# A transformer trunk on one core: norm gains applied later, fp32 router logits, and a new order of the experts' weight chunks

## The chip, the core and the metric

The kernel runs on one core of a Trainium2 chip. The metric is the device time of one execution in microseconds (us), the median over several runs. Engines are named as in the profile: PE (TensorE), DVE (VectorE), ACT (ScalarE), POOL (GpSimd), and SP, which here only issues transfers.

## What is computed

The reference is a trunk of two layers over 256 latent and 256 context tokens of width 1024. Each layer: modulation by a conditioning vector (adaLN), four token mixers, a gated merge, and a layer norm; then a channel mixer and a second layer norm. The channel mixer is a dense SwiGLU network of width 3584 in layer 0 (called FFN here) and a mixture of eight such experts in layer 1 (MoE), two per token. Layer 1 computes only the latent tokens. The part that the change touches:

```python
y, yc = _token_mixing(...)
x = _layer_norm(ALPHA * x + mod[2] * y, ln1_g[layer], ln1_b[layer])
f = _channel_mixer(x * (1.0 + mod[4]) + mod[3], layer, ...)
x = _layer_norm(ALPHA * x + mod[5] * f, ln2_g[layer], ln2_b[layer])
...
def _moe_swiglu(h, w_router, w1, w3, w2):
    top_v, top_i = lax.top_k((h @ w_router).astype(jnp.float32), TOP_K)
    gates = jax.nn.softmax(top_v, axis=-1)
    ...  # each expert's rows: (silu(h @ w1) * (h @ w3)) @ w2
```

## The kernel before, in words

**Weights.** All large weights come from memory in chunks of 512 KB (`Flow.load`, L135, issued by SP into a ring of `wr` buffers). fp32 products are made from two reduced-precision parts: ACT copies a chunk to `wh` (L266), DVE subtracts to get the rest `wl` (L253), and PE multiplies hi by hi, hi by lo and lo by hi. The operations go through small helpers, so most have a helper's line: matmul L246, transpose L250, tensor-tensor L253, tensor-scalar L258 and L260, fused L263, activation L266. The class `Flow` holds the list of steps of a stage. Before each step it issues what it can ahead: loads while a raw buffer is free, casts while a cast buffer is free and the chunk either is used within `look` steps or should have arrived by an estimate (`c.ready`). The engines take their operations in the order in which the program issues them.

**The first norm of a layer** is `out_norm` (L1412). The output projection gives four tiles of 128 tokens in layer 0 (latent and context) and two in layer 1. For each tile: half of the statistics in `second`, then `normed` (aggregate on DVE, the power -1/2 on POOL, scaling on ACT and DVE), then `third`, eight PE transposes whose results ACT and DVE scale and shift into `hraw` and split into `Bh` and `Bl`, the input of the next stage. Since that scale and shift already contain the norm's gain and bias, `x` itself is needed much later, for the residual sum; still, step `fourth` computes it there with two POOL operations on 128 x 1024 (`residual`, L799): `lnr<-lnr,gbc` and `x<-lnr,bbc`. In layer 0 a string of letters sets the order of the steps per tile: `sthrn` is second, transposes of the tile before, its residual, norm; `e` is an early half of the FFN's first matmuls.

**The FFN** (`ffn`) has seven groups of four column blocks, each with two halves of PE work. After a half, `fill(1)` lets one more block of the adaLN projection be made: two chunks, 16 small matmuls on PE or three multiply-and-add stages on POOL. `between` runs pieces of other work. `rest` ends with the final norms of the four tiles; `fill(96)` ahead of them issues what is left of the adaLN blocks.

**Router.** In layer 1 `route` multiplies the split input with the split router weights (32 matmuls per two tiles with `wrs`), copies the logits to SBUF, turns them round with four small matmuls, and takes the two largest of eight; `as_rows` turns the input back into token rows for the gather. Then counts (`pc`), positions (`pp`), the experts' order by size and the choice of one of three programs follow. SP loads the experts' first chunks (L2363) once the order is known.

**MoE.** Experts are sorted by tokens into eight slots. The run shown takes the program with 256, 192, 128, 64, 32, 32, 32, 32 tokens at most. Slots 0 to 2 are *hot*: their chunks are cast and multiplied in three products. Slots 3 to 7 are *cold*: raw fp32 chunks are used as the stationary side, in many short matmuls (`mps<-wr,Xs`, `yps<-wr,mhs`). Every slot has 84 chunks, 672 in all. `merged` puts hot and cold chunks in one sequence, two at a time: after a first run of 14 cold chunks it takes a hot pair when the summed cost is at or below the mean so far, else a cold pair. The cost of a chunk is a table by the slot's tokens: 3.75 n/128 up to 128 tokens, else 3 per full 128 and 2 for a rest. A tail that is written out by hand closes the sequence. A slot's input is gathered by matmuls with one-hot rows (`pg<-ohs` for the small slots together, `pg<-oh` for a hot slot); `need(order[0], 2)` has two of the eight column groups of the small gather made before the first chunk, the rest come between chunks.

Of the kernel before, what the change touches and what calls it, by code (L numbers as in the profile page):

```python
# [17 lines left out]
P = 128  # L18
# [65 lines left out]
class Flow:  # L84
# [9 lines left out]

    def step(self, fn, take=(), drop=None):
        self.steps.append((fn, list(take), list(take) if drop is None else list(drop)))
# [129 lines left out]
class Trunk:  # L226
# [1185 lines left out]
    def out_norm(self, l, Mh, Ml, streams, Nh, Nl, x, load, early=()):  # L1412
# [34 lines left out]
        def first(k2):  # L1447
            if k2 == 0:
                z.ps = [self.bank("SB"[t // 2], [512]) for t in range(nt)]
            for t in range(nt):  # L1450
                block(z.ps[t], t, k2, cs[0][k2])
            if k2 == 2 and l:

                for q in (z.g, z.b):
                    self.act(q, q, AF.Copy, scale=ALPHA)
# [22 lines left out]
        def normed(t):  # L1478
            z.x[t] = self.norm_rows(z.p, z.r[t], z.st[t], z.r[t])
# [18 lines left out]
        def fourth(t):  # L1498
            s, i = tiles[t]
            self.residual(z.x[t], z.g, z.b, x[s][:, i])  # L1500
# [4 lines left out]
        def last():  # L1505

            second(1, (0, 1, 2))
            raw(0, 0, (0, 0, 0, 0))
            second(1, (3,))
            raw(0, 1, (0, 0, 0, 0))  # L1510
            for h in range(2):
                high(0, h)
            normed(1)
            for h in range(2):
                low(0, h)
            raw(1, 0, LAST)
# [11 lines left out]
        else:  # L1528

            k012, k3 = (0, 1, 2), (3,)  # L1530
            ops = {"s": lambda t: second(t, k012), "t": lambda t: second(t, k3), "n": normed, "h": third, "r": fourth}
            for t in range(nt + 1):
                for o in "stn" if t == 0 else "sthrn" if t < nt else "eehr":
                    if o == "e":
                        early.pop(0)()
                    else:
                        i = t - (o in "hr")
                        step(lambda o=o, i=i: ops[o](i), cs[1] if o == "s" else [], cs[1] if (o, i) == ("t", nt - 1) else [])
            for f in early:
                f()  # L1540
# [4 lines left out]
    def ffn(self, Hh, Hl, Nh, Nl, x, during, between, late):  # L1545
# [13 lines left out]
        def up(f):  # L1559
# [21 lines left out]
            def rest():  # L1581
                step(a, cs[0:1])
                self.fill(1)
                step(b, cs[1:2])
                self.fill(1)
                between()
# [70 lines left out]
        def rest():  # L1657
# [16 lines left out]

            for i, t in enumerate((2, 3, 0, 1)):
# [7 lines left out]
            for i, f in enumerate(late):  # L1683
                if i == 4:
                    step(lambda: third(1))
                f()
            step(lambda: z.l.release())
# [9 lines left out]
    def body(self, out):  # L1697
# [109 lines left out]
        def during(g):  # L1807
# [10 lines left out]
            if g > 2 and not pieces and not hasattr(pz, "gone"):  # L1818
                pz.gone = True
                step(lambda: pz.z.pool.release())  # L1820
                pz.room = fl.more("rd", 2, 2, "left")
            if g == 7:
                pz.room()
# [5 lines left out]
        early, rest = self.ffn(Mh, Ml, Mh, Ml, x, during, between, [u[0] for u in s5u + M1.nak + M1.naq])  # L1829
        pz.room = self.out_norm(0, Mh, Ml, (0, 1), Mh, Ml, x, load, early)  # L1830
        self.todo = [z for l, i in TODO for z in self.blocks(l, i)]
# [11 lines left out]
        pz.room = self.out_norm(1, Nh, Nl, (1,), Nh, Nl, x, lambda: None, [lambda t=t: self.route(t, B.h, B.l) for t in range(2)])  # L1843
# [16 lines left out]
    def router(self):  # L1860
# [8 lines left out]

        R.w = T([8, 16], "wrs", F32R)  # L1870
        self.split(R.w[:, :, 0:8], R.w[:, :, 8:16], self.wrt)
        R.add = T([8], "radd")
        self.tt(R.add[:16], self.ident[:16, 0:8], self.ident[:16, 8:16], ALU.add)
# [7 lines left out]
    def route(self, t, Bh, Bl):  # L1881

        R, v = self.R, self.nc.vector
        c = slice(t * P, (t + 1) * P)
        if t == 0:
            R.pl = self.bank("V", [272])
        pl = R.pl
# [3 lines left out]
        if t == 0:  # L1891
            return
        lt = R.pool.tile([P, 256], F32, name="lgt")
        v.tensor_copy(lt[:16], pl[:16, 0:256])
        for t in range(2):
            self.mm(pl[:, 256 + t * 8:264 + t * 8], lt[:16, t * P:(t + 1) * P], R.add[:16], True, True)
        v.tensor_copy(R.lg, pl[:, 256:272].rearrange("p (a b) -> p a b", a=2))
        for t in range(2):
            v.max(R.mx[:, t], R.lg[:, t])
            v.max_index(R.ix[:, t], R.mx[:, t], R.lg[:, t])  # L1900
# [11 lines left out]
    def moe(self, Bh, Bl, xs, out):  # L1912
# [17 lines left out]
        self.tt(sel, m1, m2, ALU.add)  # L1930

# [8 lines left out]
        for t in range(2):  # L1940
            self.as_rows(t, Bh, Bl)
# [391 lines left out]
        def merged(caps, hot, cold):  # L2333
# [31 lines left out]
        for nm, caps, hot, cold in paths:  # L2365
            with contextlib.ExitStack() as arm:
# [13 lines left out]
                gb = []  # L2380
# [10 lines left out]
                def step():  # L2391
# [19 lines left out]
                def one(q, i, c):  # L2411
# [7 lines left out]
                    if q < 12 or q % 3 == 2:  # L2419
                        step()  # L2420
# [15 lines left out]
                need(order[0], 2)  # L2436
# [174 lines left out]
```

## Time and profile before

| | us |
|---|---|
| median of 3 runs | 2531.98 |
| lowest and highest run | 2526.71, 2532.57 |
| the profiled execution | 2521.39 |
| its span, first to last instruction | 2519.5 |
| PE busy | 2331.8 (93%) |
| DVE, ACT, POOL busy | 1337.9, 897.7, 830.5 |
| layer-0 norm / FFN / layer 1's norm and router / MoE | from about 605 / 653 / 1530 / 1567 |

The mean granted clock of TensorE is 0.969 of full. The page's busy times are averages over the whole span; PE's 93% tells little of a stage of 50 us. Times in the rows below are us from the span's start. A timeline row gives start, busy time, engine, line, operation, output <- inputs, partitions x elements and, in brackets, how long the engine was idle before and what released it; `xN` is N alike instructions in one row.

### The profile page before, as it was taken

What the parts mean: (1) busy time and instruction counts of PE and PEld (TensorE: products, weight loads), DVE (VectorE), ACT (ScalarE), POOL (GpSimd) and SP (SyncE); (2) the same over time, 40 slices, a digit from 0 to 9 for tenths busy, and PEclk for the clock granted to TensorE, in tenths of its full rate; (3) what the DMA queues carried; (4) which work ended last, traced back from release to release, by engine and by line L of the source; (5) the groups of instructions that cost most, each with busy time, mean ns of one, the idle gap of its engine ahead of it and who ended that gap; (6) DMA issues with size and microseconds to landing.
All of it is one profiled execution on the core that took longest, in us unless ns stands there. A gap on an engine that the chain in (4) does not pass through costs nothing. (4 is left out here: it accounts for less than half of the span.)

```text
span 2519.5 us, 44047 instructions
## 1 busy us (share of the span) xinstructions
PE 2331.8 (93%) x16948; PEld 1798.9 (71%) x16948; DVE 1337.9 (53%) x2132; ACT 897.7 (36%) x1477; POOL 830.5 (33%) x1646
## 2 busy tenths in 40 slices
PE   7799999998899999998898887999999999999995
PEld 5566666876777778777776685667777777777663
DVE  4455564346424545567465647224444465557775
ACT  2533333323322422223343444222233333345561
POOL 5307883332132565552488754000000000000000
PEclk9999998999999999998998998999999999999998
DMA  7644112324343554451332342899999999999996
GB/s 269 207 134 139 52 58 71 106 82 167 102 143 128 168 185 171 156 182 49 103 126 68 96 163 84 319 361 395 384 397 388 398 348 362 395 380 404 407 408 273
DMA packets 167995, 556.21 MB, mean 221 GB/s; under 512 B 17472, under 2 KB 32608, under 8 KB 167776
## 3 DMA queue, kind: packets, MB, share of 16 engines
q1 hardware_dynamic: 156224, 543.33, 58.6%
q10 hardware_dynamic: 11552, 9.98, 1.2%
q8 instruction: 135, 2.21, 0.4%
q14 instruction: 84, 0.69, 0.1%
HBM read 543.32 MB, written 9.92 MB: 220 GB/s over the span
## 5 line engine op out<-in xcount | busy, mean ns | idle before, releaser
L253 DVE TENSOR_TENSOR wl<-wr,wh 128x1024 fp32r<-128x1024 f32 (+1 forms) x412 | 529.6, 1304 | 353.1 <-ACT wh L266 350.2
L266 ACT ACTIVATE wh<-wr 128x1024 fp32r<-128x1024 f32 x474 | 493.0, 1052 | 475.3 <-DMA wr<-in_moe_w_dram 264.1
L253 POOL TENSOR_TENSOR wide<-ymo,mbc 32x128 f32<-32x128 f32 (+1 forms) x28 | 18.7, 668 | 586.9 <-DVE ymo L253 522.3
L253 POOL TENSOR_TENSOR wl<-wr,wh 128x1024 fp32r<-128x1024 f32 x62 | 151.5, 2458 | 168.9 <-ACT wh L266 161.3
L246 PE MATMUL psA<-Bh,wh 128*128 128x256 f32 (+1 forms) x592 | 204.3, 345 | 1.3 <-ACT gt L266 1.3
L246 PE MATMUL psA<-Bh,wl 128*128 128x256 f32 (+1 forms) x592 | 197.7, 334 | 0.5 <-DVE wl L253 0.5
L246 PE MATMUL psA<-Bl,wh 128*128 128x256 f32 (+1 forms) x592 | 198.0, 334 | 0.0
L246 PE MATMUL mps<-wr,Xs 128*32 128x128 f32 (+1 forms) x4032 | 177.2, 290 | 9.2 <-DMA wr<-in_moe_w_dram 6.6
L246 PE MATMUL mps<-wh,X 128*128 128x512 f32 x560 | 179.9, 406 | 2.5 <-ACT wh L266 2.5
L246 PE MATMUL yps<-wh,mh 128*128 128x512 f32 x504 | 162.4, 403 | 2.4 <-ACT wh L266 2.3
L246 PEld LDWEIGHTS mps<-wr,Xs 128*32 128x32 f32 (+1 forms) x4032 | 122.8, 113 | 56.8 <-issue 23.8
L253 POOL TENSOR_TENSOR t<-H,a 128x32 f32<-128x32 f32 x512 | 151.0, 316 | 21.8 <-PE psV L246 2.3
L246 PE MATMUL psA<-Hh,wh 128*128 128x512 f32 x352 | 151.4, 430 | 6.4 <-ACT wh L266 5.4
L246 PE MATMUL psA<-Hl,wh 128*128 128x512 f32 x352 | 144.0, 409 | 0.0
L246 PE MATMUL psA<-Hh,wl 128*128 128x512 f32 x352 | 143.8, 408 | 0.1
L246 PEld LDWEIGHTS psA<-Bh,wh 128*128 128x128 f32 x592 | 116.2, 196 | 25.5 <-issue 6.8
L246 PE MATMUL psB<-wh,hid 128*128 128x512 f32 x384 | 123.1, 402 | 7.7 <-DVE y L253 7.7
L246 PEld LDWEIGHTS mps<-wh,X 128*128 128x128 f32 x560 | 102.2, 189 | 33.6 <-issue 5.0
L246 PEld LDWEIGHTS psA<-Bh,wl 128*128 128x128 f32 x592 | 115.9, 196 | 11.6 <-DVE wl L253 0.8
L246 PEld LDWEIGHTS psA<-Bl,wh 128*128 128x128 f32 x592 | 116.3, 196 | 9.8 <-issue 0.2
L246 PE MATMUL mps<-wl,X 128*128 128x512 f32 (+1 forms) x336 | 118.9, 402 | 4.0 <-DVE wl L253 3.9
L246 PEld LDWEIGHTS yps<-wh,mh 128*128 128x128 f32 x504 | 92.1, 188 | 29.9 <-ACT wh L266 4.9
(515 smaller groups left out, 4820.2 us busy)
## 6 DMA issues: line engine op xcount, KB each, us to landing
wr<-in_moe_w_dram SPq DMA_DIRECT2D x672, 512.0 KB, 8.0
wr<-in_w_ada_dram SPq DMA_DIRECT2D x96, 512.0 KB, 4.4
wr<-in_ffn_w_dram SPq DMA_DIRECT2D x84, 512.0 KB, 4.4
wr<-in_w_gate_dram SPq DMA_DIRECT2D x64, 512.0 KB, 3.5
wr<-in_w_in_dram SPq DMA_DIRECT2D x28, 512.0 KB, 3.7
wr<-in_w_branch_dram SPq DMA_DIRECT2D x16, 512.0 KB, 3.5
wr<-in_w_out_dram SPq DMA_DIRECT2D x16, 512.0 KB, 3.5
wr<-in_w_v_dram SPq DMA_DIRECT2D x8, 512.0 KB, 5.1
```

What stands on the lines that cost most here:

```text
L246: self.nc.tensor.matmul(out, w, x, start=start, stop=stop)
L253: (eng or self.nc.vector).tensor_tensor(out, a, b, op=op)
L266: self.nc.scalar.activation(out, a, f, **kw)
```

## The change

Five things change.

- **Residual of the first norms.** `normed` writes the normalised tile straight into `x`; the gain and bias rows are not loaded in `out_norm`. In layer 0 eight POOL operations on 128 x 1024 apply them to `x` inside the FFN, one with each `between`, after the pieces of the S5 work. In layer 1 two rows are loaded at the MoE's chunk 24 into the space that slot 2's input takes later, and at chunk 40 two ACT scalings and four POOL operations apply them; slot 2's gather may begin from chunk 120.
- **adaLN blocks.** `fill(2)` stands three times among the layer-0 norm steps (letter `f`), and the FFN fills only from its fifth column block on.
- **Quiet stretches.** In the layer-0 norms and in the FFN's final norms, a chunk that is first used more than ten steps later is not cast early.
- **Router.** Logits come from the unsplit `hraw` (fp32) and the unsplit router weights, 16 matmuls into 128 x 8, before the splits; copies and the turning matmuls go. `as_rows(0)` stands before the counts, `as_rows(1)` behind them.
- **MoE order.** The cost is 3.5 n/128 below 128 tokens (128 tokens cost 3), the first cold run is 6 chunks, and all eight column groups of the small gather are made before the first chunk.

```diff
@@ Flow.ahead
-                if c.raw or (r and (c.first <= self.now + self.look or self.tr.clock >= c.ready)):
+                if c.raw or (r and (c.first <= self.now + self.look or self.tr.clock >= c.ready and not self.later(c))):
...
+    def later(self, c):
+        return any(a <= self.now < b and c.first > self.now + 10 for a, b in self.quiet)
@@ out_norm
-            z.g, z.b = (p.tile([P, D], F32, name=n) for n in ("gbc", "bbc"))
-            self.rows(z.g, A['ln_rows'][l, 0])
-            self.rows(z.b, A['ln_rows'][l, 1])
...
         def normed(t):
-            z.x[t] = self.norm_rows(z.p, z.r[t], z.st[t], z.r[t])
+            s, i = tiles[t]
+            z.x[t] = self.norm_rows(z.p, z.r[t], z.st[t], x[s][:, i])
...
             raw(0, 1, (0, 0, 0, 0))
+            early[0]([z.raw[0, h] for h in range(2)])
...
             raw(1, 1, LAST)
-            early[0]()
+            early[1]([z.raw[1, h] for h in range(2)])
...
-            early[1]()
-            for t in range(2):
-                fourth(t)
...
-                for o in "stn" if t == 0 else "sthrn" if t < nt else "eehr":
+                for o in "stn" if t == 0 else "sthn" if t < nt - 1 else "stfhn" if t < nt else "eefhfee":
                     if o == "e":
                         early.pop(0)()
+                    elif o == "f":
+                        self.fill(2)
@@ ffn
-                self.fill(1)
+                self.fill(f > 3)
@@ body, during
+                for s in range(2):
+                    for i in range(2):
+                        for h, op in enumerate((ALU.mult, ALU.add)):
+                            pieces.append(lambda s=s, i=i, h=h, op=op: self.tt(x[s][:, i], x[s][:, i], pz.gb[h], op, nc.gpsimd))
@@ route
-        for k in range(8):
-            self.mm(pl[:16, c], R.w[:, k], Bh[:, k, c], k == 0, False)
-            self.mm(pl[:8, c], R.w[:, k, 0:8], Bl[:, k, c], False, k == 7)
...
+        for h, raw in enumerate(raws):
+            for k in range(4):
+                self.mm(R.pl[:, t], raw[:, k], self.wrt[:, h * 4 + k], h + k == 0, h + k == 4)
+        v.tensor_copy(R.lg[:, t], R.pl[:, t])
@@ moe
-                return 3.75 * n / P if n <= P else 3 * (n // P) + 2 * (n % P > 0)
+                return 3.5 * n / P if n < P else 3 * (n // P) + 2 * (n % P > 0)
-                i = 1 if len(seq) < 14 else 0 if sm <= mean * len(seq) else 1
+                i = 1 if len(seq) < 6 else 0 if sm <= mean * len(seq) else 1
...
+                        if s == 2 and q < 120:
+                            return
...
+                    if q == 40:
+                        for i, op in enumerate((ALU.mult, ALU.add)):
+                            self.act(ab[0][:, i], ab[0][:, i], AF.Copy, scale=ALPHA)
+                            for t in range(2):
+                                self.tt(xs[:, t], xs[:, t], ab[0][:, i], op, g)
...
-                need(order[0], 2)
+                need(order[0], 8)
```

DVE in the layer-0 norms, at tile 3 of 0 to 3, before: `lns` holds a tile's half statistics, `lnm` its mean and factors, `wl` is a weight chunk's low part, `Bl` the split of the tile before.

```order
L754 BN_STATS lns<-lnr_5499 128x6
L253 TENSOR_TENSOR wl<-wr,wh 128x1024 x3
L260 TENSOR_SCALAR hraw<-psB,affG,affB 128x128
L253 TENSOR_TENSOR Bl<-hraw,Bh 128x4x128
L260 TENSOR_SCALAR hraw<-psB,affG,affB 128x128
L253 TENSOR_TENSOR Bl<-hraw,Bh 128x4x128
L760 BN_AGGR lnm<-lns 128x2
```

And the same place with the change (its helpers' lines are 5 higher):

```order
L759 BN_STATS lns<-lnr_5495 128x6
L258 TENSOR_TENSOR wl<-wr,wh 128x1024
L265 TENSOR_SCALAR hraw<-psB,affG,affB 128x128
L258 TENSOR_TENSOR Bl<-hraw,Bh 128x4x128
L265 TENSOR_SCALAR hraw<-psB,affG,affB 128x128
L258 TENSOR_TENSOR Bl<-hraw,Bh 128x4x128
L765 BN_AGGR lnm<-lns 128x2
```

Two of the three casts stand behind the aggregate now.

DVE in the layer-1 norm, from tile 1's half statistics to the indices of the two largest logits, before:

```order
L754 BN_STATS lns<-lnr_14142 128x6
L760 BN_AGGR lnm<-lns 128x2
L258 TENSOR_SCALAR lnm<-lnm 128x1
L263 SCALAR_TENSOR_TENSOR lnm<-lnm 128x1
L260 TENSOR_SCALAR lnr_14142<-lnr_14142,lnm 128x512
L253 TENSOR_TENSOR Bl<-hraw,Bh 128x4x128 x2
L260 TENSOR_SCALAR hraw<-psB,affG,affB 128x128 x2
L253 TENSOR_TENSOR Bl<-hraw,Bh 128x4x128 x2
L1894 COPY lgt<-psV 16x256
L1897 COPY lg<-psV 128x16
L1899 MAX mx_14132<-lg 128x8
L1900 MAX_INDEX ix_14133<-mx_14132,lg 128x8
```

With the change:

```order
L759 BN_STATS lns<-lnr_14138 128x6
L1898 COPY lg<-psV 128x8
L1899 MAX mx_14132<-lg 128x8
L1900 MAX_INDEX ix_14133<-mx_14132,lg 128x8
L765 BN_AGGR lnm<-lns 128x2
L263 TENSOR_SCALAR lnm<-lnm 128x1
L268 SCALAR_TENSOR_TENSOR lnm<-lnm 128x1
L265 TENSOR_SCALAR x_5483<-lnr_14138,lnm 128x512
L258 TENSOR_TENSOR Bl<-hraw,Bh 128x4x128 x2
L265 TENSOR_SCALAR hraw<-psB,affG,affB 128x128 x2
L1898 COPY lg<-psV 128x8
L1899 MAX mx_14132<-lg 128x8
```

Tile 0's logits stand ahead of tile 1's aggregate, tile 1's ahead of the last two splits.

PE at the start of the MoE, before (`pg<-ohs` is the gather of the small slots, `pg<-oh` that of slot 0, `mps` a chunk's products):

```order
L246 MATMUL pg<-ohs,Bl 128x192 x2
L246 MATMUL mps<-wr,Xs 64x256 x4
L246 MATMUL pg<-ohs,Bh 128x192 x2
L246 MATMUL pg<-ohs,Bl 128x192 x2
L246 MATMUL pg<-ohs,Bh 128x192 x2
L246 MATMUL pg<-ohs,Bl 128x192 x2
L246 MATMUL mps<-wr,Xs 64x256 x4
```

With the change, from the last of eight such column groups:

```order
L251 MATMUL pg<-ohs,Bh 128x192 x2
L251 MATMUL pg<-ohs,Bl 128x192 x2
L251 MATMUL mps<-wr,Xs 64x256 x12
L251 MATMUL pg<-oh,Bh 128x256 x2
L251 MATMUL pg<-oh,Bl 128x256 x2
L251 MATMUL mps<-wr,Xs 64x256 x4
```

The eight column groups stand ahead of the first chunk.

## Rows read from the trace of the kernel before

**Rows 1.** Windows, four stretches: us, PE, PEld, DVE, ACT, POOL busy, PEclk, DMA share, GB/s.
```profile
605.00:653.00 48.00, 31.19 (x178) 27.70 (x177) 36.57 (x51) 22.05 (x41) 23.20 (x12) 0.86 0.18 55
...
1530.00:1587.00 57.00, 38.21 (x194) 29.49 (x192) 33.26 (x83) 16.23 (x35) 11.75 (x7) 0.70 0.37 140
...
1740.00:2270.00 530.00, 521.95 (x5590) 394.14 (x5588) 269.13 (x351) 191.78 (x248) 20.40 (x25) 1.00 0.98 382
...
2270.00:2490.00 220.00, 202.43 (x1914) 147.54 (x1913) 156.01 (x187) 110.35 (x129) 4.82 (x8) 1.00 1.02 407
```

**Rows 2.** Timeline, layer-0 norms, PE: start, us, operation, [idle before <-releaser].
```profile
611.19 1.97 PE L250 MATMUL psB<-in_small_dram,lnr 128*128 128x128 f32 x8 [5.58 <-ACT lnr L266]
...
621.09 1.10 PE L250 MATMUL psB<-in_small_dram,lnr 128*128 128x128 f32 x8 [1.99 <-ACT lnr L266]
...
630.12 1.18 PE L250 MATMUL psB<-in_small_dram,lnr 128*128 128x128 f32 x8 [2.41 <-ACT lnr L266]
...
645.25 1.97 PE L250 MATMUL psB<-in_small_dram,lnr 128*128 128x128 f32 x8 [6.83 <-ACT lnr L266]
```

**Rows 3.** Timeline, layer-0 norms, DVE and POOL at tiles 2 and 3.
```profile
631.43 2.37 POOL L253 TENSOR_TENSOR lnr<-lnr,gbc 128x1024 f32<-128x1024 f32 x1 [2.41 <-PE psB L250]
...
631.77 7.59 DVE L253 TENSOR_TENSOR wl<-wr,wh 128x1024 fp32r<-128x1024 f32 x3
...
633.89 3.25 POOL L253 TENSOR_TENSOR x<-lnr,bbc 128x1024 f32<-128x1024 f32 x1
...
646.18 1.22 DVE L253 TENSOR_TENSOR wl<-wr,wh 128x1024 fp32r<-128x1024 f32 x1 [1.25 <-ACT wh L266]
```

**Rows 4.** Windows, late FFN; timeline, POOL, the last adaLN block and the final norm's power.
```profile
1000.00:1070.00 70.00, 68.38 (x304) 55.43 (x303) 39.41 (x39) 18.27 (x21) 43.14 (x32) 1.00 0.49 171
...
1131.29 2.90 POOL L253 TENSOR_TENSOR wr<-wr,csil 128x1024 f32<-128x1024 f32 x1
...
1138.17 0.45 POOL L253 TENSOR_TENSOR ada<-wr 128x128 f32<-128x128 f32 x1
...
1146.62 0.57 POOL L253 TENSOR_TENSOR lnm<-lnm,mhalf 128x1 f32<-128x1 f32 x1 [8.00 <-DVE lnm L258]
```

**Rows 5.** Timeline, DVE at layer 0's first tile, then layer-1 norm and router.
```profile
610.13 0.16 DVE L263 SCALAR_TENSOR_TENSOR lnm<-lnm 128x1 f32<-128x1 f32 x1 [0.66 <-POOL lnm L253]
...
610.32 0.55 DVE L260 TENSOR_SCALAR lnr<-lnr,lnm 128x512 f32<-128x512 f32 x1
...
1547.69 2.29 DVE L263 SCALAR_TENSOR_TENSOR lnm<-lnm 128x1 f32<-128x1 f32 x1 [0.67 <-POOL lnm L253]
...
1550.01 2.66 DVE L260 TENSOR_SCALAR lnr<-lnr,lnm 128x512 f32<-128x512 f32 x1
...
1556.11 3.53 DVE L253 TENSOR_TENSOR Bl<-hraw,Bh 128x512 fp32r<-128x512 f32 x2
...
1559.70 0.27 PE L246 MATMUL psV<-Bl,wrs 128*8 128x128 f32 x1 [2.11 <-DVE Bl L253]
...
1564.02 0.56 PE L246 MATMUL pc<-sel,onesr 128*128 128x8 f32 x2 [1.89 <-DVE sel L253]
```

**Rows 6.** Timeline, PE, the first chunk and the fourth (of the four).
```profile
1573.88 1.98 PE L246 MATMUL mps<-wr,Xs 128*64 128x256 f32 x8 [0.72 <-DVE Xs L2086]
...
1587.50 2.81 PE L246 MATMUL mps<-wr,Xs 128*64 128x256 f32 x24 [0.58 <-ACT Xs L266]
```

**Rows 7.** Timeline, PE, chunks of 64, 32 and 192 tokens (two from 2002.23).
```profile
1712.52 5.40 PE L246 MATMUL mps<-wr,Xs 128*64 128x256 f32 x48
...
1806.44 1.95 PE L246 MATMUL mps<-wr,Xs 128*32 128x128 f32 x64
...
2002.23 0.73 PE L246 MATMUL mps<-wh,X 128*128 128x512 f32 x2
...
2007.09 1.08 PE L246 MATMUL yps<-wr,mhs 128*32 128x128 f32 x32
```

**Rows 8.** Waits of SP's queue, 1560 to 2519 us: total, times, longest.
```profile
SPq L135 <- PE mps L246: 189.3, 129, 9.8
```

More of the change, by code (lines that the diff above doesn't have):

```diff
@@ L93, in __init__ @@
         self.pre = pre
+        self.quiet = []
     def step(self, fn, take=(), drop=None):
@@ L1451, in first @@
                 block(z.ps[t], t, k2, cs[0][k2])
-            if k2 == 2 and l:
-                for q in (z.g, z.b):
-                    self.act(q, q, AF.Copy, scale=ALPHA)
             if k2 == 3:
@@ L1496, in low @@
             self.tt(lo, src, hi.bitcast(F32), ALU.subtract)
-        def fourth(t):
-            s, i = tiles[t]
-            self.residual(z.x[t], z.g, z.b, x[s][:, i])
         z.x, z.raw = {}, {}
@@ L1530, in out_norm @@
             k012, k3 = (0, 1, 2), (3,)
-            ops = {"s": lambda t: second(t, k012), "t": lambda t: second(t, k3), "n": normed, "h": third, "r": fourth}
+            ops = {"s": lambda t: second(t, k012), "t": lambda t: second(t, k3), "n": normed, "h": third}
+            a = len(self.flow.steps)
             for t in range(nt + 1):
-                for o in "stn" if t == 0 else "sthrn" if t < nt else "eehr":
+                for o in "stn" if t == 0 else "sthn" if t < nt - 1 else "stfhn" if t < nt else "eefhfee":
                     if o == "e":
                         early.pop(0)()
+                    elif o == "f":
+                        self.fill(2)
                     else:
-                        i = t - (o in "hr")
+                        i = t - (o in "h")
                         step(lambda o=o, i=i: ops[o](i), cs[1] if o == "s" else [], cs[1] if (o, i) == ("t", nt - 1) else [])
-            for f in early:
-                f()
+            self.flow.quiet.append((a, len(self.flow.steps)))
         step(lambda: z.p.release())
@@ L1686, in rest @@
                 f()
+            self.flow.quiet.append((a, len(self.flow.steps)))
             step(lambda: z.l.release())
@@ L1821, in during, with rows @@
                 pz.room = fl.more("rd", 2, 2, "left")
+                def rows():
+                    pz.gp = self.pool("ln0")
+                    pz.gb = [pz.gp.tile([P, D], F32, name=n) for n in ("gbc", "bbc")]
+                    for h in range(2):
+                        self.rows(pz.gb[h], A['ln_rows'][0, h])
+                step(rows)
+                for s in range(2):
+                    for i in range(2):
+                        for h, op in enumerate((ALU.mult, ALU.add)):
+                            pieces.append(lambda s=s, i=i, h=h, op=op: self.tt(x[s][:, i], x[s][:, i], pz.gb[h], op, nc.gpsimd))
+                            if h:
+                                pieces.append(lambda: None)
+                pieces.append(lambda: pz.gp.release())
             if g == 7:
@@ L1829, in body @@
         early, rest = self.ffn(Mh, Ml, Mh, Ml, x, during, between, [u[0] for u in s5u + M1.nak + M1.naq])
+        self.todo = [z for l, i in TODO for z in self.blocks(l, i)]
         pz.room = self.out_norm(0, Mh, Ml, (0, 1), Mh, Ml, x, load, early)
-        self.todo = [z for l, i in TODO for z in self.blocks(l, i)]
         rest()
@@ L1842, in body @@
         step(self.router)
-        pz.room = self.out_norm(1, Nh, Nl, (1,), Nh, Nl, x, lambda: None, [lambda t=t: self.route(t, B.h, B.l) for t in range(2)])
+        pz.room = self.out_norm(1, Nh, Nl, (1,), Nh, Nl, x, lambda: None, [lambda raws, t=t: self.route(t, raws) for t in range(2)])
         pz.room()
@@ L1879, in router, with route @@
         R.lg, R.mx, R.ix = T([2, 8], "lg"), T([2, 8], "mx8"), T([2, 8], "ix8", U32)
-    def route(self, t, Bh, Bl):
+    def route(self, t, raws):
         R, v = self.R, self.nc.vector
-        c = slice(t * P, (t + 1) * P)
         if t == 0:
-            R.pl = self.bank("V", [272])
-        pl = R.pl
-        for k in range(8):
-            self.mm(pl[:16, c], R.w[:, k], Bh[:, k, c], k == 0, False)
-            self.mm(pl[:8, c], R.w[:, k, 0:8], Bl[:, k, c], False, k == 7)
[L1891 to L1900, printed above, removed]
+            R.pl = self.bank("V", [2, 8])
+        for h, raw in enumerate(raws):
+            for k in range(4):
+                self.mm(R.pl[:, t], raw[:, k], self.wrt[:, h * 4 + k], h + k == 0, h + k == 4)
+        v.tensor_copy(R.lg[:, t], R.pl[:, t])
+        v.max(R.mx[:, t], R.lg[:, t])
+        v.max_index(R.ix[:, t], R.mx[:, t], R.lg[:, t])
     def as_rows(self, t, Bh, Bl):
@@ L1939, in moe @@
         self.mm(pp[:, 1], self.ones, sf[:, 0], False, True)
-        for t in range(2):
-            self.as_rows(t, Bh, Bl)
+        self.as_rows(1, Bh, Bl)
         pos, key, slot = T([2, 8], "pos"), T([8], "key"), T([8], "slot")
@@ L2389, in moe, with step @@
                 todo.insert(0 if order[0] in small else len(todo), (None, setup_small(small)))
-                def step():
+                def step(q):
                     if todo:
                         s = todo[0][0]
+                        if s == 2 and q < 120:
+                            return
                         if s is None or s in slots:
@@ L2419, in one @@
                     if q < 12 or q % 3 == 2:
-                        step()
+                        step(q)
+                    if q == 24:
+                        last = "X2" if caps[2] == P else "X3"
+                        ab.append(pool.tile([P, caps[2] // 64, D], F32, name="ab", tag=last, bufs=1))
+                        for i in range(2):
+                            self.rows(ab[0][:, i], A['ln_rows'][1, i])
+                    if q == 40:
[3 more added lines that the diff above has]
+                                self.tt(xs[:, t], xs[:, t], ab[0][:, i], op, g)
                     for _ in jobs[:1 if q < len(seq) - 8 else 3 * (q < len(seq) - 1)]:
```

10 lines of the change are left out of this document (4 added, 6 removed).

## Prediction

> **What bounds the kernel now.** I read the windows view first, stage by stage, since TensorE's 93% of the whole span hides where it waits. [Rows 1] are the four stretches that the change touches. In the layer-0 norms (605 to 653 us) PE works 31.2 of 48 us, in the layer-1 norm and router (1530 to 1587 us) 38.2 of 57: there PE waits for a chain of small DVE, ACT and POOL operations. In the experts (MoE) PE works 522 of 530 us up to 2270, while the transfers run at 382 GB/s [rows 1]; from 2270 to 2490 it works only 202 of 220 us and the transfers run at 407 GB/s, the most that they reach. So the first stretch of the experts is PE's, the last the transfers'. Then I read the timeline of each stretch for the operations that end PE's waits, and at last the price of one chunk of each kind on PE.
>
> Against those windows a difference of 0.3% (7.6 us) is about what a measurement of this kernel can tell from no change.
>
> **Layer-0 norms.** PE waits four times, each time before the eight transposes of a normed tile: 5.58, 1.99, 2.41 and 6.83 us [rows 2], 16.8 in sum. The first stays: nothing is put in front of it. Ahead of the other three DVE works through splits and weight casts while POOL runs the residual. What that costs stands in [rows 3]: three `wl` casts took 7.59 us beside the two POOL operations (2.37 and 3.25 us), one took 1.22 alone; 7.59 − 3 × 1.22 = 3.9 us more, and tile 3's statistics wait in DVE's queue behind all three. The change takes the POOL pair out, lets two of the three casts come later (the order excerpt shows one in place of three) and puts a block of adaLN matmuls into the waits of tiles 2 and 3. So tile 3's statistics come 3.9 + 2 × 1.22 = 6.4 us sooner, and its wait falls from 6.83 to about 0.4; tile 2's 2.41 is filled by the block; tile 1's 1.99 falls to about 0.5, since its two splits no longer run beside POOL. That is 6.4 + 2.4 + 1.5 = 10.3; with the clock, which stands at 0.86 in this window, a little more: **−11**. Ends: −14 (all three waits and 3 us of clock) and −6 (tile 3 alone). The adaLN blocks' own PE time only changes place.
>
> **Residual in the feed-forward network (FFN).** The eight POOL operations (4 tiles × 2, 2.37 to 3.25 us [rows 3], about 20 us) come in the last groups. POOL is busy 43 of 70 us there while PE works 68.4 of 70 [rows 4]: POOL's 27 free us take the 20, and what covers them is the casts' lead over PE. **+1**, ends 0 and +4 (two late casts of some 2 us). The two loads of gain and shift only move; there SP has transfers at 171 GB/s, well under 407, and they cost nothing. Without the casts' lead each operation would cost what it blocks on DVE: that is the second rival.
>
> **End of the FFN.** Fewer adaLN blocks are issued in groups 0 to 3, so two stand directly ahead of the final norms. One block on POOL lasted from 1131.29 to 1138.62, 7.3 us [rows 4]. POOL then lay idle for 8.00 us before the first tile's power at 1146.62: one more block is covered, the second ends about 14.6 − 8.0 = 6.6 us late. PE, in order, then meets the transposes that wait for that norm. Ends 0 and +6; PE had matmuls between, and I take the middle, **+3**.
>
> **Layer-1 norm and router.** Beside POOL's residual a tiny DVE step took 2.29 us and a half-tile scaling 2.66 [rows 5]; the same forms take 0.16 and 0.55 at 610 us in layer 0 [rows 5]. With no residual there, up to 4.2 us fall away, part of it behind ACT's half of the same tile, so 2. The last two `Bl` splits took 3.53 us, and PE's router matmuls waited 2.11 for them [rows 5]. Now the logits come from the raw tile ahead of the splits: that wait, the copies and the second matmul go, some 4 us between 1556 and the counts at 1564.02. Against it, tile 0's logits, maximum and index now stand on DVE ahead of tile 1's aggregate (order excerpt), and the rows' transposes stand on PE ahead of the counts, behind the splits. **−6**; ends −8 and −2 (the splits become the end of the chain again).
>
> **Start of the experts.** Four small gathers alternate with chunks; PE waited 0.72 us before the first chunk and 0.58 before the fourth, four times about 0.65, 2.6 in sum [rows 6]. With all eight column groups gathered first, those waits overlap the next gather: **−2.6**; ends −3 and +3 (the first chunk starts three gathers later, and buffers come free later; from 1573.88 to 1587.50 there are three rounds of a chunk of 1.98 us, a wait and a gather, so a gather takes 4.54 − 1.98 − 0.65 = 1.9 us, and half of 5.7 may be lost).
>
> **The chunks' order.** A chunk of 512 KB lasts 0.524288 MB / 407 GB/s = 1.29 us in transfer [rows 1]. On PE two chunks of the 192-token expert lasted from 2002.23 to 2007.09, 2.43 each; four of a 32-token expert took 1.95, 0.49 each; six of the 64-token expert 5.40, 0.90 each [rows 7]. So an order keeps both PE and transfers full if its mean is 1.29 us. Counting the order of the change against that of before over the first 504 of 672 chunks: 72 instead of 80 of the 192-token expert, 264 instead of 256 of 32 tokens, the rest alike. PE has 8 × (2.43 − 0.49) = 15.5 us less to do in the part that it bounds. The part's transfers lost 530 × (1 − 382/407) = 33 us, so there is room for it. In the last 168 chunks PE gets the same 15.5 us: 202.4 + 15.5 = 218 against 168 × 1.29 = 217 us of transfers. That is just full, so I take 2.5 us back: **−13**. Ends: −22 (two thirds of the 33 lost) and +5 (the tail runs at 18 us of waits as before, and a little of the head's gain fails). The two added loads of gain and shift are 1 MB, 2.6 us of transfer, but only took another place: layer 1's norm read the same rows before. Slot 2's gather only moves; ACT's two scalings move too, off the norm.
>
> The Trainium skill, "DMA: Bandwidth & Descriptors", section "Where 436 GB/s comes from", says that for transfers from HBM the limit of about 358 GB/s per core binds. By that, an estimate, the 672 chunks could not take less than 984 us, and no order would be worth anything; the 407 GB/s over 220 us of [rows 1] disagree, and the row decides.
>
> **Sum.** −11 + 1 + 3 − 6 − 2.6 − 13 = −28.6 us. The profiled execution took 2521.4 us; 2492.8 after. The median of the three runs is 2532.0, 10.6 above it, so the forecast for the median is **2503 us**.
>
> **Rivals.**
> 1. The order gives nothing: what leaves the head fills the tail, and the sum of transfers and the start decide. For it: the tail would be full on PE and transfers alike, with casts on DVE as a third (SP waited 189 us for buffers held by PE's `mps` matmuls [rows 8], and denser busy chunks hold them longer). Against it: the head's 522 of 530. Then −28.6 + 13 = −15.6: 2516.
> 2. Slower: the twelve POOL operations that were moved (8 into the FFN, 4 into the experts) hold up DVE, and PE waits each time. For it: [rows 3, 5], some 2 us of DVE per operation. Against it: DVE's casts run ahead of PE in both stages. It decides if PE waits over (28.6 + 7.6) / 12 = 3.0 us at each, about the whole of an operation; at 3.25 us each it is +39, less the 1 already counted: 2541.
> 3. The change doesn't do what it says. The costs in the order's table: 3.5 × 64/128 = 1.75 for 64 tokens, 0.875 for 32 and 5 for 192; by [rows 7], with 2.43 us as 5, they would be 1.85 and 1.01, so the table still holds quiet chunks for cheaper than they are; and the adaLN blocks may find their weights not yet there and leave the waits of layer 0 as they are. Layer 0's norms and the order then give a third of their 24 each, and 16 are lost: −28.6 + 16 = −13: 2519.
>
> Beside the second: the Trainium skill, "SBUF — State Buffer", section "SBUF: two separate sides", says that VectorE with two SBUF inputs and GpSimd hold a shared port pair as an exclusive lock for the whole instruction. It speaks against moving such operations beside casts; the 2.29 us of a step of 0.16 agree with blocking.
>
> **How the numbers follow.** Forecast 0.50 (own range 2488 to 2514), first rival 0.20, third 0.14, second 0.06; 0.10 for several terms failing at once, which ends within 7.6 us of now or above. The best ends sum to −14 − 8 − 3 − 22 = −47, 2485; the worst without the second rival to −6 + 4 + 6 − 2 + 3 + 5 = +10. The range reaches from **2485** to **2526**. Faster by over 0.3% (below 2524.4): 0.50 + 0.19 + 0.11 = 0.80; within: 0.12; slower: 0.08.
>
> **What would show it.** Right: PE's waits before the transposes of tiles 2 and 3 under 1 us each; no DVE step over 2 us near the layer-1 norm; in the experts over 390 GB/s between 1740 and 2270, and PE over 95% busy in the last 220 us. Wrong: an unchanged rate there with the tail longer (first rival); PE waiting `<-DVE wl` by 30 us or more in the FFN (second); the four waits of the layer-0 norms as they stand (third).

## The result and the profile after

The change took 2491.1 us (median of 4 runs, 2484.9 to 2503.8) against 2532.3 for the kernel before (4 runs, 2526.7 to 2539.3): a ratio of 0.985, 95% interval 0.9811 to 0.9889, so 28 to 48 us less. The forecast was 2503, the range 2485 to 2526.

The profiled execution of the change is its slowest run: 2503.76 us, span 2501.9. It must be read by stage, since it lies 15 us behind the profile of before already when the first changed instruction comes. I measured the stages between events that both programs have: the four aggregates of the layer-0 norms on DVE, those of the FFN's norms, the first aggregate of layer 1, the first issue of an expert chunk, the last landing, the end. Beside it stand all the other executions of this study whose code in that stage is the one of before; the rows with 12 also take in kernels in which two small loads or the experts' order differ.

| stage, us | before | executions with that code | change |
|---|---|---|---|
| start to layer 0's first aggregate | 609.1 | 602.0 to 622.3 (12) | 624.0 |
| first to fourth aggregate | 34.1 | 34.0 to 34.3 (4) | 25.1 |
| to the first of the FFN's norms | 503.0 | 498.2 to 505.4 (4) | 506.4 |
| first to fourth of those | 39.9 | 39.4 to 39.9 (4) | 41.5 |
| to layer 1's first aggregate | 353.3 | 352.2 to 360.3 (12) | 354.2 |
| to the first issue of an expert chunk | 28.0 | 27.1 to 28.5 (4) | 20.5 |
| to the last landing | 931.5 | 930.1 (1) | 909.7 |
| to the end | 20.6 | 20.5 to 21.1 (12) | 20.5 |

Among the five executions with exactly the code of before the first row moves by 17 us (605.1 to 622.3), so the 15 us fit the spread of executions. Against the means of the rows' executions the stages that changed differ by −9.0, +5, +2, −7.2 and −21: −30 us in sum, inside the interval of the runs. The medians differ by 41 us; the 11 us between the two are not traced to a stage. (In two later runs with the change's code there, the FFN took 505.1 and 506.0 us and its norms 38.7 and 39.2, so the +2 is not the change's.) The change's experts, in five later executions with the same code there, took 909.5 to 915.0 us: single executions of that stage are no finer than some 5 us.

The windows view of the change, over the stretches that answer to [rows 1] (us, busy time of PE, PEld, DVE, ACT, POOL, granted clock, DMA share, GB/s):

```profile
620.00:668.00 48.00, 41.63 (x354) 37.25 (x353) 30.44 (x61) 25.49 (x47) 2.19 (x4) 0.96 0.31 100
1545.00:1590.00 45.00, 36.52 (x211) 31.22 (x211) 27.98 (x87) 18.98 (x39) 1.11 (x2) 0.73 0.38 146
1744.00:2275.00 531.00, 522.04 (x5758) 394.80 (x5760) 267.94 (x357) 189.02 (x249) 21.80 (x29) 1.00 1.00 391
2275.00:2482.00 207.00, 197.29 (x1801) 150.01 (x1793) 158.12 (x190) 112.81 (x128) 2.52 (x2) 0.98 1.01 398
```

PE works 41.6 of 48 us in the layer-0 norms instead of 31.2 (some of it is the adaLN blocks that now stand there). In the experts PE is as full as before, but the transfers run at 391 GB/s instead of 382, and the stage as a whole is some 21 us shorter (the table above).

PE's timeline in the layer-0 norms, the transposes of tiles 0, 2 and 3 that answer to [rows 2] (tile 1's has no wait left):

```profile
626.09 1.36 PE L255 MATMUL psB<-in_small_dram,x 128*128 128x128 f32 x8 [4.63 <-ACT x L271]
...
642.42 1.09 PE L255 MATMUL psB<-in_small_dram,x 128*128 128x128 f32 x8 [0.71 <-ACT x L271]
...
651.24 1.09 PE L255 MATMUL psB<-in_small_dram,x 128*128 128x128 f32 x8 [1.02 <-ACT x L271]
```

The waits of 1.99, 2.41 and 6.83 us are 0, 0.71 and 1.02.

The end of the FFN is where time was lost. POOL, DVE and PE there:

```profile
1135.15 2.75 DVE L268 SCALAR_TENSOR_TENSOR y<-x,y 128x1024 f32<-128x1024 f32 x1
1136.90 3.80 POOL L258 TENSOR_TENSOR wr<-wr 128x512 f32<-128x512 f32 x2
1137.83 2.29 DVE L258 TENSOR_TENSOR y<-y,mbc 128x1024 f32<-128x1024 f32 x1
...
1140.78 1.32 POOL L258 TENSOR_TENSOR ada<-wr 128x128 f32<-128x128 f32 x1
...
1143.10 0.14 DVE L258 TENSOR_TENSOR mod<-psV,in_small_dram 128x1 f32<-128x1 f32 x1
...
1143.39 0.56 PE L251 MATMUL psV<-ones,ada 128*128 128x1 f32 x2 [5.05 <-DVE mod L258]
...
1145.71 0.55 PE L251 MATMUL psV<-ones,ada 128*128 128x1 f32 x2 [1.76 <-DVE mod L258]
```

PE's sum of an adaLN block (`psV<-ones,ada`) waits until DVE has taken the sum before it out of PSUM (`mod`), and that small step stands in DVE's queue behind the wide `y` steps, which run beside POOL's adaLN work. They take 2.75 and 2.29 us here; in the run no_fill below, the same two forms took 1.23 and 1.22 us once POOL had stopped. PE waits 5.05 and 1.76 us.

Layer 1's norm and router, answering to [rows 5]:

```profile
1552.32 0.16 DVE L268 SCALAR_TENSOR_TENSOR lnm<-lnm 128x1 f32<-128x1 f32 x1 [0.73 <-POOL lnm L258]
...
1552.52 0.55 DVE L265 TENSOR_SCALAR x<-lnr,lnm 128x512 f32<-128x512 f32 x1
...
1562.33 3.48 PE L251 MATMUL psV<-in_small_dram,hraw 128*128 128x8 f32 x16
...
1566.41 1.27 DVE L258 TENSOR_TENSOR Bl<-hraw,Bh 128x512 fp32r<-128x512 f32 x2
...
1568.32 0.59 PE L251 MATMUL pc<-sel,onesr 128*128 128x8 f32 x2
```

The steps of 2.29, 2.66 and 3.53 us take 0.16, 0.55 and 1.27.

### The profile page after: what moved, and what is told of

The parts are those of the page before. It is cut to its first block, busy times and chain, and to the rows that moved or that the text cites. A ratio compares the mean times of both kernels' runs of the same rounds, so it can differ in the third digit from the quotient of the medians.

```text
span 2501.9 us, 44047 instructions
## 1 busy us (share of the span) xinstructions
PE 2331.8 (93%) x16944; PEld 1807.9 (72%) x16944; DVE 1329.8 (53%) x2128; ACT 897.8 (36%) x1476; POOL 833.1 (33%) x1648
## 5 line engine op out<-in xcount | busy, mean ns | idle before, releaser
L258 POOL TENSOR_TENSOR t<-H,a 128x32 f32<-128x32 f32 x512 | 145.4, 304 | 21.7 <-PE psV L251 2.3
L271 ACT ACTIVATE prb<-psS,mx 128x512 f32<-128x512 f32 (+1 forms) x96 | 58.3, 612 | 156.9 <-DVE mx L263 156.9
```

Source lines behind the costliest of these rows:

```text
L258: (eng or self.nc.vector).tensor_tensor(out, a, b, op=op)
L271: self.nc.scalar.activation(out, a, f, **kw)
```

## Experiments

My theory after the result: the gain is the absence of POOL's residual beside DVE in both norms, and in the experts the order, as PE's work; the adaLN blocks' new places cost more than they bring. Rivals: the early casts or the plain logits did the work in the norms; transfers bound the experts, and the start or the cover of the norms did the rest.

### The three edits of the experts, alone and together

**cost_only**: the new prices alone.

```diff
-                return 3.75 * n / P if n <= P else 3 * (n // P) + 2 * (n % P > 0)
+                return 3.5 * n / P if n < P else 3 * (n // P) + 2 * (n % P > 0)
```

> The kernel before with the new cost table alone (first cold run 14, two column groups before the first chunk, as before). I read the time from the first issue of an expert chunk to the last landing: 931.5 us in the trace of before, 909.7 in that of the change. If the table does it (8 chunks of the 192-token expert leave the first 504 chunks, 15.5 us of PE work), 913 to 920 us here, and the run is 12 to 18 us faster than before. If the transfers alone decide, or the start does it, 928 to 934 us and no difference above 0.3%.

**start_only**: the first run and the gathers alone.

```diff
-                i = 1 if len(seq) < 14 else 0 if sm <= mean * len(seq) else 1
+                i = 1 if len(seq) < 6 else 0 if sm <= mean * len(seq) else 1
-                need(order[0], 2)
+                need(order[0], 8)
```

> The kernel before with the first cold run of 6 chunks and all eight column groups of the small gather before the first chunk, old cost table. If the table does it, the time from first issue to last landing falls by the four waits of 0.6 to 0.7 us alone, 928 to 932 us against 931.5, within 0.3% of before. If the start does most of it, 915 us or less.

**order_only**: the edits of both.

> The kernel before with all three edits of the MoE (table, first run, gathers), nothing of norms, router or adaLN. If what the change gained in the experts is these edits and does not hang on the rest, first issue to last landing is 907 to 913 us (909.7 with the whole change) and the run is 16 to 22 us faster than before. If the two scalings and four POOL operations moved into the experts cost something there, it is shorter here than 907.

| | first issue to last landing | issue of chunk 60, 440 and the last, after the first issue | ratio to before |
|---|---|---|---|
| before | 931.5 | 89.3, 616.6, 921.9 | |
| cost_only | 922.2 | 90.1, 601.8, 912.2 | 0.9939 (0.9906 to 0.9972) |
| start_only | 924.8 | 84.5, 608.7, 914.7 | 0.9971 (0.9947 to 0.9995) |
| order_only | 909.1 | 84.0, 593.3, 899.0 | 0.9904 (0.9865 to 0.9944) |
| change | 909.7 | 84.0, 592.6, 899.4 | 0.985 (0.9811 to 0.9889) |

All that the change gains in the experts is these edits; the two scalings and four POOL operations that were moved there cost nothing that shows (909.7 against 909.1). The table on top of the start is worth 15.4 us at chunk 440 and 15.7 at the last one, so there the tail gives nothing back. Alone it has 14.8 us at chunk 440, but only 9.7 at the end: 922.2 us, above the 913 to 920 that I expected. It stood 3.4 us longer at the lower clock after chunk 440, which is a small part of that; the rest is open. So the two edits gain more together (22.4 us) than one by one (9.3 + 6.7), and why is open.

The forecast's 15.5 us belong to chunk 504, not 440. By the 440th chunk only six 192-token chunks have left (48 instead of 54 in the order that the program makes), which would be 6 × (2.43 − 0.49) = 11.6 us. At the 504th, where it is eight, the issue came 14.6 us sooner on top of the start (681.7 against 696.3 us) and 13.9 alone (690.9 against 704.8).

The start was a miss: I expected the four waits of 2.6 us and it brought 6.7 against the first profile of before, 5.3 against the second, and 4.8 of them by chunk 60. The windows view of the first 25 us from about the first issue, before and start_only:

```profile
1567.00:1592.00 25.00, 20.28 (x117) 14.15 (x116) 8.28 (x35) 6.93 (x15) 0.95 (x1) 0.67 0.84 317
```

```profile
1564.00:1589.00 25.00, 22.99 (x147) 18.94 (x147) 12.82 (x45) 10.90 (x21) 0.95 (x1) 0.76 0.91 352
```

PE works 2.7 us more, the four waits, and its granted clock is 0.76 instead of 0.67 of full (1.2 and 2.4 GHz are its two levels). The first 60 chunks are the same in both kernels, in another order. Over them PE is busy 82.5 of 84.5 us instead of 84.6 of 89.3, and stands 10.8 us at the lower level instead of 16.0. An estimate: 5.2 us less at half speed are worth 2.6, and with the 2.7 of the waits that is 5.3, about the 4.8 us found. So waits and clock cover the gain up to there. Whether the clock rose sooner because the pauses between gathers are gone, or because of the shorter first run, no run here separates.

### The kernel before, once more

> The kernel before once more, for the spread of its stages from one execution to another. Start to the first aggregate of layer 0's norms was 609.1 us, first to fourth aggregate 34.1, then 503.0 to the first aggregate of the FFN's norms, 39.9 to its fourth, 353.3 to the first of layer 1, 28.0 to the first expert chunk's issue, 931.5 to the last landing. If the 15 us that the change's profile lies behind before its first changed instruction are the execution's own, the first number moves by some 5 to 15 us here too and the later ones by 2 or less.

622.3, 34.0, 498.2, 39.9, 357.5, 27.1 and 930.1 us. The stages up to layer 0 and the mixers of layer 1 go with the clock of the execution (55 us at the lower level before layer 0's norms here, 34 in the first profile); the other stages agree within 5 us in 500 and within 1.5 elsewhere. The FFN's 4.8 us and the mixers' 4.2 are more than the 2 us that I had allowed for.

### What the norms gained from

**residual_only**: the kernel before with the residual's new place and nothing else (the diff shows the norm; the operations in the FFN and the experts are the change's).

```diff
         def normed(t):
-            z.x[t] = self.norm_rows(z.p, z.r[t], z.st[t], z.r[t])
+            s, i = tiles[t]
+            z.x[t] = self.norm_rows(z.p, z.r[t], z.st[t], x[s][:, i])
```

> Only the residual's gain and bias moved out of both first norms (8 POOL operations in the FFN, 4 in the experts); adaLN blocks, early casts, router and order as before. If POOL beside DVE is what stretched the norms: layer 0 from the first to the fourth aggregate 34.1 us becomes 28 to 30 (25.1 with the whole change), layer 1 from its first aggregate to the first expert issue 28.0 (27.1 to 28.5 in the runs with these stages unchanged) becomes 23 to 25, and PE shows no new wait in the FFN where the eight operations run. If the early casts in DVE's queue were the cause, layer 0 stays above 32. If the moved operations hold up DVE's casts (second rival of the prediction), the FFN from 498 to 505 us grows by 10 or more.

Layer 0 took 26.9 us, layer 1 21.2, less than I expected of both; the FFN took 500.3. Its DVE timeline where [rows 3] had three casts of 7.59 us in sum, and where [rows 5] had two splits of 3.53:

```profile
621.59 3.48 DVE L258 TENSOR_TENSOR wl<-wr,wh 128x1024 fp32r<-128x1024 f32 x3
...
1535.94 1.29 DVE L258 TENSOR_TENSOR Bl<-hraw,Bh 128x512 fp32r<-128x512 f32 x2
```

The same instructions in the same order, with no POOL beside them. What POOL did in layer 1 before, beside the DVE steps of [rows 5]:

```profile
1547.62 2.34 POOL L253 TENSOR_TENSOR lnr<-lnr,gbc 128x1024 f32<-128x1024 f32 x1
...
1550.04 2.35 POOL L253 TENSOR_TENSOR x<-lnr,bbc 128x1024 f32<-128x1024 f32 x1
...
1556.42 2.68 POOL L253 TENSOR_TENSOR x<-lnr,bbc 128x1024 f32<-128x1024 f32 x1
```

The residual's place is 7.2 of the 9.0 us in layer 0 and 6.8 of 7.5 in layer 1 (against the first profile). PE's wait of 2.11 us for `Bl` is 0.49 here. The eight operations in the FFN brought one new wait of 0.89 us, about 121 us before the stage's end, and the four in the experts none that shows (928.4 us with the old order): the second rival falls.

**no_quiet**: the change without the rule on early casts.

```diff
-        return any(a <= self.now < b and c.first > self.now + 10 for a, b in self.quiet)
+        return False
```

> The change without the rule that keeps far casts out of the norm steps. If the two later casts were worth what they last, layer 0 from first to fourth aggregate is 25.1 + 2 x 1.22 = 27.5 us, and the wait before tile 3's transposes 3 us or more instead of 1.02. If without POOL beside it the casts fit into DVE's free time, 25 to 26 us.

26.3 us, between the two, and the wait before tile 3 was 2.15 us. The edit brought back only one of the two casts: at tile 3 DVE has `wl` x2 (2.34 us) where the change has one (1.21) and before had three. A better pair is residual_only and no_fill (below), whose layer-0 norms differ in this rule alone: from the third aggregate to the fourth 11.08 us with three casts and 8.81 with one. That is 2.27 us for two casts, what they last. The FFN of this run took 511.4 us, 5 more than the change's; it has the change's waits at the end, stood 23.9 us at the lower clock against the change's 17.1, and PE idled 22.8 us against 20.4. Whether the rule has a share in that, one execution does not show.

**router_old**: the change with the split logits of before.

```diff
-                self.mm(R.pl[:, t], raw[:, k], self.wrt[:, h * 4 + k], h + k == 0, h + k == 4)
+            self.mm(pl[:16, c], R.w[:, k], Bh[:, k, c], k == 0, False)
+            self.mm(pl[:8, c], R.w[:, k, 0:8], Bl[:, k, c], False, k == 7)
```

> The change with the router of before (split logits, copies, turning matmuls; row transposes behind the positions). Layer 1 from its first aggregate to the first expert issue is 20.5 us with the change, 27.1 to 28.5 before. If plain logits are worth the 4 us that I gave them, 24 to 25 us here; if the residual's absence did nearly all, 21 to 22; if the router did all, 27 to 28.

21.7 us, and residual_only, which has the old router too, 21.2; so the plain logits and the earlier row transposes together are worth 0.7 to 1.2 us. The 16 fp32 matmuls of tile 1 took 3.48 us at a granted clock of 0.50 (the timeline above), while the split ones wait only for splits that no longer run beside POOL.

### The adaLN blocks

**no_fill**: the change with the blocks where they were; and the same kernel again, timed, as **no_fill_timed**.

```diff
-                for o in "stn" if t == 0 else "sthn" if t < nt - 1 else "stfhn" if t < nt else "eefhfee":
+                for o in "stn" if t == 0 else "sthn" if t < nt else "eehee":
-                self.fill(f > 3)
+                self.fill(1)
```

> The change with the adaLN blocks where they were before: none in the layer-0 norms, one credit after every half of the FFN from its start. If the new waits at the end of the FFN (5.05 and 1.76 us before the sums of adaLN blocks) come from the two blocks that now stand there, they are gone, and the stage from layer 0's fourth aggregate to the first of the FFN's norms falls from 506.4 us to about 500. Layer 0's waits before tiles 2 and 3 then grow from 0.71 and 1.02 us by at most 1 us each, if the blocks were not needed to fill them, or by 1.5 to 2.4 each if they were.

> The change with the adaLN blocks where they were before, timed (its one look: 2478.0 us). The stages say 8 us less than the change: 5 at the end of the FFN, 2.5 in its norms, 0.5 in layer 0. Then the ratio to before is 0.981 to 0.983, against 0.985 for the change. If the blocks in the norms were worth their place after all, it is above 0.985.

The FFN took 501.2 and 500.6 us instead of 506.4, its norms 39.0 and 39.9, layer 0 24.6 both times. The ratio of no_fill_timed to before is 0.9822 (0.9791 to 0.9854), its median 2484.5 us. The waits in layer 0 and the adaLN sums at the end of the FFN in the first of the two:

```profile
615.87 1.09 PE L255 MATMUL psB<-in_small_dram,x 128*128 128x128 f32 x8 [1.27 <-ACT x L271]
623.80 1.09 PE L255 MATMUL psB<-in_small_dram,x 128*128 128x128 f32 x8 [1.32 <-ACT x L271]
632.61 1.09 PE L255 MATMUL psB<-in_small_dram,x 128*128 128x128 f32 x8 [2.02 <-ACT x L271]
...
1128.47 0.72 PE L251 MATMUL psV<-ones,ada 128*128 128x1 f32 x6
```

Without the blocks PE waits some 3 us more in layer 0, yet the aggregates follow each other no slower: the blocks filled waits with work that PE had room for elsewhere. At the end of the FFN the sums wait for nothing. All four executions with the change's places (the change, no_quiet, router_old, less_pe) have the wait of 5.05 to 5.07 us; none of the four with the blocks placed otherwise has it.

**fill_from3**: the blocks stay in the norms, the FFN starts its own one column block sooner.

```diff
-                self.fill(f > 3)
+                self.fill(f > 2)
```

> The change with the FFN's adaLN blocks starting one column block sooner (two credits more), so that none is left for the end; those in the layer-0 norms stay. If the 5.05 and 1.76 us of waits come from where the last two blocks stand, and not from the blocks in the layer-0 norms, they vanish here too: from layer 0's fourth aggregate to the first of the FFN's norms 499 to 502 us instead of 506.4, and the stage sum equals that of the kernel with the old places. If the FFN simply holds too few free us on POOL, the wait stays near 5.

498.7 us and 39.6 in the norms; the ratio is 0.9814 (0.9771 to 0.9857), 2483.5 us. So the waits came from the two blocks left for the FFN's end, and not from those in the norms. Both variants have less time than the change by these stages (8 to 10 us against its profile, 6 to 7 against the mean of that and the two later runs with its code), and by their medians; against the change itself the intervals overlap.

### What bounds the experts

**less_pe**: one of three products of the hot chunks is left out.

```diff
                     self.mm(p, xh, wh[:, kk], k == 0, False)
-                    self.mm(p, xl, wh[:, kk], False, False)
                     self.mm(p, xh, wl[:, kk], False, k == 2 * n2 - 1)
```

> The change without one of the three products of the hot chunks in the experts (low part of the tokens times high part of the weights, in every full tile of 128 tokens), which is left out of the computation: 4 matmuls fewer per chunk of slot 0, 2 per chunk of slots 1 and 2, 84 x 0.93 + 168 x 0.47 = 157 us less on PE; casts and transfers as they are. If PE is what bounds most of the experts' 909.7 us from first issue to last landing, they fall until the transfers bind: 672 x 1.29 = 866 us and some 20 of the start, 883 to 892 us. If transfers bind already (first rival of the prediction), or the casts do, they stay above 902.

883.2 us from first issue to last landing. Its windows:

```profile
1740.00:2270.00 530.00, 469.51 (x5626) 340.17 (x5625) 283.38 (x374) 198.53 (x258) 17.88 (x29) 0.98 1.03 406
2270.00:2450.00 180.00, 148.32 (x1282) 94.30 (x1284) 138.12 (x162) 99.86 (x116) 2.51 (x2) 0.96 1.02 404
```

PE is busy 778.2 us of the stage instead of 886.9, 109 less and not the 157 that I had priced; it stands some 60 us at the lower clock against 21, and idles 105. The transfers run at 406 GB/s instead of 391 from 1740 on, and SP's queue waits longest for the transfers themselves (190.7 us); with the change it waited longest for PE's `mps` (200.9). So in the change PE still costs the experts 26.5 us. What sets the 883 us is mostly the transfers and the start; the queue also waits 133.5 us for DVE's casts, so that an order alone could gain all of the 26.5 is not shown. With cost_only and order_only, the first rival falls.

**no_fill_costs**: the no_fill kernel with cold prices as the rows give them.

```diff
-                return 3.5 * n / P if n < P else 3 * (n // P) + 2 * (n % P > 0)
+                return {32: 1.02, 64: 1.85}[n] if n in (32, 64) else 3 * (n // P) + 2 * (n % P > 0)
```

> The change with the adaLN blocks where they were before and with the prices that the rows give for cold chunks (1.02 for 32 tokens, 1.85 for 64, in place of 0.875 and 1.75). It takes 2 more chunks of the 192-token expert out of the first 504 and 2 of the 256-token one out of the first 336. If the table's remaining error matters (third rival of the prediction), first issue to last landing falls by 3 us or more from 910; if head and tail are balanced by now, it stays within 2 us.

912.7 us, against 910.2 and 915.0 without it; the ratio is 0.9824 (0.9787 to 0.9861), like no_fill_timed. The table's remaining error is worth nothing that shows here.

## Why the prediction was right

The time lay in the range, 12 us below the forecast. By stages the sum is −30 us against −28.6, and that this is so close is partly luck: the experts gained 5.5 us more than forecast, and the layer-0 norms and the FFN with its end came out 5 worse. The range itself is not drawn as its text says: the worst ends sum to +10, which is 2542, and the prediction gives no reason for stopping at 2526. Of its signs, the wait before tile 3 missed narrowly (1.02 us, under 1 asked); the others came (391 GB/s, PE 95% busy in the last 207 us, no DVE step over 1.3 us near the layer-1 norm). Point by point:

- **Layer-0 norms**, −11 forecast, −9.0 measured. The mechanism holds: casts and splits stretched by POOL. From aggregate to aggregate tile 3 gained 6.3 us (15.12 to 8.81, forecast 6.4), tile 1 2.0 (forecast 1.5) and tile 2 0.6 (forecast 2.4). The mis-sized part is the adaLN block in tile 2's wait: without any block tile 2 gained 1.2 (no_fill), and residual_only has the waits of tiles 1 and 2 at 1.29 and 1.33.
- **Residual in the FFN**, +1: one new wait of 0.89 us (500.3 us in all in residual_only, 498.2 to 505.4 before).
- **End of the FFN**, +3 with an upper end of 6; some +5 measured (no_fill against the change), but the step failed in its place. I had the norm's power late on POOL and the transposes waiting. The wait came one step sooner: the adaLN sum waits for DVE's `mod`, and DVE is slowed beside POOL. I followed POOL's queue and not DVE's, so the size came near by luck.
- **Layer-1 norm and router**, −6 forecast, −7.2 to −7.5 measured, the shares wrong: 2 us for the residual and 4 for the logits became 6.8 and about 1. The 2.11 us that PE waited for `Bl` I counted as the split's; most of it, 1.6 us, was POOL's operation on top of it (0.49 in residual_only).
- **Start of the experts**, −2.6 forecast, −5 to −7 measured: the waits are there, 2.7 us, but the term left out PE's clock, which stood 5.2 us less at its lower level over the first 60 chunks.
- **Order**, −13 forecast, 15.7 measured at the end on top of the start, 9.3 alone against the first profile of before, 8 against the second. Of the 15.5 us that I worked out from 8 × (2.43 − 0.49), 13.9 to 14.6 stood at chunk 504. The 2.5 us that I took back for a full tail did not appear on top of the start; alone the tail took back about 4.

The two rules of the Trainium skill can now be set against more rows. "SBUF — State Buffer", section "SBUF: two separate sides", has the second of GpSimd and a VectorE operation with two SBUF inputs to come blocked until the first one ends. This case agrees within 0.02 us: before the change DVE's step of 0.16 us began at 1547.69, took 2.29 [rows 5] and so ended at 1549.98, when POOL's operation of 2.34 us, begun at 1547.62, had ended at 1549.96. The next DVE step, a scaling with one wide input, is outside the rule as told here: it began at 1550.01, 0.03 us ahead of POOL's second operation, and still took 2.66 us instead of 0.55. "DMA: Bandwidth & Descriptors", section "Where 436 GB/s comes from", holds about 358 GB/s to bind transfers from HBM; less_pe moved 406 GB/s over 530 us, so that figure is no ceiling here.

## What to carry to other kernels

A wide POOL operation beside a chain of small DVE steps can cost the chain nearly its full length (2.29 us for a step of 0.16), even if POOL itself is mostly idle: move it to a stage whose DVE work runs ahead of PE, and look there for small DVE steps that PE waits for. When two streams share an order, price the pieces by the trace and count the work that leaves the part that PE bounds; that count was right within 1 to 2 us at the chunk that it was made for. And ask of each filler not whether it fits a wait, but whether its old place was free: here it was. The blocks in the norms bought nothing that shows, and the two that were left for the FFN's end cost some 5 us there.

## What I had not expected of the hardware

Four waits of 0.6 to 0.7 us at the start of the experts went together with 5 to 7 us: the granted clock of the first 25 us was 0.67 with them and 0.76 without. And the same code ahead of layer 0's norms took 605 to 622 us from one execution to the next, with 31 to 55 us of them at the lower clock: single runs cannot tell terms of 5 us apart. Short stages between events of the trace can (the layer-0 norms of before took 34.0 to 34.3 us in five executions); long ones, as the FFN and the experts, repeat within some 5 to 7 us only.
